# Alternating plain and seven-product k-groups in both feed-forwards, with later flips and 40 low parts made by ACT and an accumulating DMA

## The chip, the cores and the metric

One core of a Trainium2 chip runs the kernel. The metric is the device time in microseconds (us) of one execution; three executions gave a median of 2728.22 us. The profile is of one more execution.

## What is computed

Two transformer-like blocks on 256 tokens of width 2048, all in float32, one after the other. Cut to what the change touches:

```python
def swiglu(h, w_gate, w_up, w_down):                    # first block, hidden width 5632
    return (jax.nn.silu(h @ w_gate) * (h @ w_up)) @ w_down

def conv_glu_ffn(h, w_up, conv_w, conv_b, w_down):      # second block, hidden width 5632
    u = h @ w_up                                        # 2 x 5632 columns
    u = causal_depthwise_conv(u, conv_w) + conv_b       # 3 taps along the tokens
    gate, val = u[..., :5632], u[..., 5632:]
    return (jax.nn.silu(gate) * val) @ w_down
```

The first block is attention and `swiglu`, the second a gated mixer, a cross attention and `conv_glu_ffn`, each with a residual add and an RMS norm in front.

## The kernel before, in words

**Units, tasks and chunks.** Every weight matrix is cut into units of 512 rows by 512 columns (1 MB, one DMA on SP's queue into one of 4 `raw` buffers). The order of all units is fixed beforehand by `plan`. A unit is used as two *tasks* of 256 rows. For each task `split_ahead` makes two tiles: `wh`, the weights rounded to the short float format that TensorE multiplies fast (a cast on ACT, L225), and `wl`, what the rounding left (weights minus `wh`, a subtraction on DVE, L226). There are 5 buffers of each. `task()` calls `split_ahead` three tasks ahead of the one that TensorE takes. One product of activations and weights is three matmuls (`mm`, L270 to L272): high by high, high by low, low by high. A k-group is 512 rows of the shared dimension (4 of 128), a chunk is 512 output columns. An ordinary task is 12 matmuls of 512 columns: 2 row blocks of 128, 2 outputs, 3 matmuls.

**The pair.** In the first feed-forward, chunks 1 to 10 of gate and up are computed together by `pair`. Gate and up columns, token halves and row halves form 2 by 2 blocks. A *plain* k-group costs 48 matmuls in 4 tasks. A *seven-product* k-group does the same block product with 7 instead of 8 products (Strassen's scheme in Winograd's form): 42 matmuls in 7 tasks of 6, but DVE must first form the sums of weights, in place in `raw` (`form`, L242, L243, L244, L246, four instructions), and all 7 operands need their own cast and subtraction. Sums of activations are made once by `differences`. Before the change k-groups 0, 1, 2 are plain and 3 is seven-product. At the end DVE adds the partial products (L359 to L373), ACT applies silu (L787), DVE multiplies (L774), and `group_job` flips the result: TensorE transposes (L405) and a split into high and low part (L387, L388). The second feed-forward uses the ordinary `gemm` for its up chunks, then `conv_job`: flips (L405), taps (L1139, L1140, L1142), silu, product, split.

**What is done when.** TensorE's instructions run in the order of the program text. The order on the other engines is a scheduler's, which takes what is ready. Side jobs (`spawn`) are advanced by `tick`, once after every 6 matmuls of the projections. `group_job` and `conv_job` wait 3 ticks before their first flip. After each part of up chunks (`PARTS1`, `PARTS2`) the down projection of the part before runs: four column chunks n, each adding into `x` (`add_x`, L451).

**Memory.** PSUM has 4 banks `acc`, 3 `aux` (flips, and in `pair` one product each) and one `po`. SBUF tiles come from tags with a fixed number of buffers (`s4` 21, `s2` 12).

Of the kernel before, what the change touches and what calls it, by code (L numbers as in the profile page):

```python
# [83 lines left out]
class _Net:  # L84
# [71 lines left out]
    def units(w, n, ks=range(4)):  # L156
        return [(w, n, k) for k in ks]

    def plan(self):

        p, U = [], self.units
        self.seven = set()
# [10 lines left out]
        def ffn(gate, up, off, down, parts, seven=False):  # L173
            prev = None
            for ks in parts:
                for c in ks:
                    if seven and c:
                        pair(U(gate, c), U(up, c + off))
                    else:
                        add([U(gate, c), U(up, c + off)], c == 0)  # L180
                if prev:
                    add([U(down, n, prev) for n in range(4)])
                prev = ks
            add([U(down, n, prev) for n in range(4)])

        add([U("w_qkv", n) for n in (4, 0, 1, 2, 3)])
        add([U("w_o", n) for n in range(4)], True)
        ffn("w_gate", "w_up1", 0, "w_dn1", PARTS1, True)
# [9 lines left out]
        ffn("w_up2", "w_up2", 11, "w_dn2", PARTS2)  # L198
        return p

    def load_ahead(self, n):
# [10 lines left out]
    def split_ahead(self, n):  # L212

        nc = self.nc
        while self.halves < min(n, len(self.tasks)):
            u, j = self.tasks[self.halves]
            if j < 10:
                self.load_ahead(u + 1)
                raw = self.raws[u][:, 2 * j:2 * j + 2]
            else:  # L220
                raw = self.form(u, j - 10)
            h = self.wp.tile([128, 2, 512], F32R, name=self.nm("wh"), tag="wh", bufs=WBUF)
            l = self.wp.tile([128, 2, 512], F32R, name=self.nm("wl"), tag="wl", bufs=WBUF)
            for m in (slice(0, 1), slice(1, 2)) if u == 0 else (slice(0, 2),):
                nc.scalar.copy(h[:, m], raw[:, m])  # L225
                nc.vector.tensor_sub(l[:, m], raw[:, m], h[:, m].bitcast(F32))  # L226
            self.parts[self.halves] = (h, l)
            self.halves += 1
            if j == 1:
                del self.raws[u]  # L230
                self.load_ahead(u + 1 + RAW)
            elif j == 16:
                del self.raws[u], self.raws[u + 1], raw
                self.load_ahead(u + 2 + RAW)
# [53 lines left out]
                    done(banks[c])  # L288
                self.tick()

    def differences(self, acts):


        nc = self.nc
# [1 line left out]
        for g, z in enumerate(acts):  # L296
# [2 lines left out]
            nc.vector.tensor_add(f, h.bitcast(F32), l.bitcast(F32))  # L299
            p, q = f[:, :, 0:128], f[:, :, 128:256]  # L300
            yield 2
            if g < len(acts) - 1:
                hl = self.s4([128, 2, 4, 128], F32R)
                nc.vector.tensor_sub(p, p, q)
                nc.scalar.copy(hl[:, 0], p)
                nc.vector.tensor_sub(hl[:, 1], p, hl[:, 0].bitcast(F32))
                out.append((hl[:, 0], hl[:, 1]))
            else:
                s = self.s4([128, 8, 128])
                nc.vector.tensor_add(s[:, 0:2], q[:, 0:2], q[:, 2:4])  # L310
                nc.vector.tensor_sub(s[:, 2:4], s[:, 0:2], p[:, 0:2])
                nc.vector.tensor_sub(s[:, 4:6], p[:, 0:2], q[:, 0:2])
                nc.vector.tensor_sub(s[:, 6:8], p[:, 2:4], s[:, 2:4])
                yield 1
                h, l = (self.s4([128, 8, 128], F32R) for _ in range(2))
                nc.scalar.copy(h, s)
                nc.vector.tensor_sub(l, s, h.bitcast(F32))
                out.append((h, l))
            yield 2
        return out  # L320

    def pair(self, left, right, acts, diffs):

        nc = self.nc
        acts = [self.need(z) for z in acts]
        p2, p4, p5, p3 = (self.bank(tag="acc") for _ in range(4))
        last = len(acts) - 1  # L330
        for g in range(last):
            for units in (right, left):
                for k, w in enumerate(self.weights(units[g])):
                    f = g == 0 and k == 0
                    if units is left:
                        self.mm(p2, acts[g], k, 0, w, f, False)
                        self.mm(p4, acts[g], k, 1, w, f, False)
                    else:
                        self.mm(p5, acts[g], k, 1, w, f, False)
                        self.mm(p3, diffs[g], k, 0, w, f, False)  # L340
                    self.tick()
        assert self.stream[self.used:self.used + 2] == [right[last], left[last]]
        self.used += 2
        A, S = acts[last], diffs[last]

        def product(o, z, k, t, start):
            h, l = self.task()
            for i in range(2):
                self.mm(o, z, k + i, t, (h[:, i], l[:, i]), start and i == 0, i == 1)
            self.tick()  # L350

        add = nc.vector.tensor_add
        u, a, b, c = (self.s2([128, 512]) for _ in range(4))
        product(p3, S, 6, 0, False)
        o = self.bank()
        product(o, A, 0, 0, True)
        nc.scalar.copy(u, o)
        product(p2, A, 2, 0, False)
        add(a, p2, u)  # L359
        yield a  # L360
        o = self.bank()
        product(o, S, 2, 0, True)
        add(u, o, u)
        product(p5, S, 0, 0, False)
        add(b, p5, u)
        add(b, p3, b)
        yield b
        o = self.bank(tag="po")
        product(o, S, 4, 0, True)
        add(u, o, u)  # L370
        product(p4, A, 2, 1, False)
        add(c, p4, u)
        add(u, p5, u)  # L373
        yield c
        yield u
# [384 lines left out]
    def swiglu(self):  # L760
        nc, a = self.nc, self.a
        r, xacts = self.r, self.xacts

        def up(c, late):
            silu, hid = [], []

            def on_gate(G):
# [4 lines left out]
            def on_up(U):  # L772
                for t in range(2):
                    nc.vector.scalar_tensor_tensor(silu[t], U[t], r[:, t:t + 1], silu[t],  # L774
                                                   op0=ALU.mult, op1=ALU.mult)
                hid.append(self.spawn(self.group_job(silu)))

            if c == 0:
                self.gemm([(self.units(w, c), f) for w, f in (("w_gate", on_gate), ("w_up1", on_up))],
                          xacts, late=late)  # L780
                diffs.append(self.spawn(self.differences(xacts)))
                return hid[0]
            diffs[0] = self.need(diffs[0])
            U = []
            for i, z in enumerate(self.pair(self.units("w_gate", c), self.units("w_up1", c), xacts, diffs[0])):
# [4 lines left out]
            return hid[0]  # L790

        diffs = []
        self.ffn(up, "w_dn1", PARTS1, lambda *z: self.residual(*z, "g_mix_2"))

    def ffn(self, up, w, parts, last):

        prev = None
        for p in parts:
            hid = [up(c, late=c == 0) for c in p]
            if prev:  # L800
                self.residual(w, *prev, None)
            prev = (p, hid)
        last(w, *prev)


    def mixer(self):
# [320 lines left out]
    def conv_ffn(self):  # L1127
# [16 lines left out]
            return y  # L1144

        def conv_job(c, rows):
            yield 3
            hl = self.group()
            for k in (0, 2):
                yg = conv(rows[0], c, k)  # L1150
# [5 lines left out]
                yield 1  # L1156
            return hl

        def up(c, late):
            rows, hid = [], []  # L1160

            def on_gate(p):
# [2 lines left out]
            def on_val(p):  # L1165
# [1 line left out]
                hid.append(self.spawn(conv_job(c, rows)))  # L1167

            self.gemm([(self.units("w_up2", c + 11 * j), f)
                       for j, f in enumerate((on_gate, on_val))], xacts, late=late)  # L1170
            return hid[0]

        self.ffn(up, "w_dn2", PARTS2, self.final)

    def final(self, w, ks, acts):

# [115 lines left out]
```

## Time and profile before

| what | value |
|---|---|
| median of 3 executions | 2728.22 us (2726.79 to 2728.71) |
| profiled execution | 2726.57 us |
| its span, first to last instruction | 2724.7 us |
| TensorE busy | 2684.9 us (99%) |
| DVE / ACT / POOL busy | 1669.1 / 1354.5 / 27.1 us |
| mean granted TensorE clock | 0.999 of 2.4 GHz |

Matmuls overlap, and their ends are modelled, so a busy TensorE says little; the spacing of what waits for it says more. Idle time of DVE, ACT or the queues costs nothing unless TensorE waits for it. The profiled execution has 1.9 us outside its span.

### The profile page before, as it was taken

How to read it: one execution, taken by the hardware profiler on the slowest of the kernel's cores; microseconds unless marked ns; L12 is line 12 of the kernel's file. 1: busy time of each engine (PE TensorE's matmuls, PEld its weight loads, DVE VectorE, ACT ScalarE, POOL GpSimd, SP SyncE). 2: the span in 40 equal slices, each digit the busy share in tenths (PEclk: the TensorE clock that was granted, in tenths of full speed). 3: DMA queues.
4: the chain of work that ended last, by engine and by line, in shares of the span. 5: the costliest groups of instructions: out<-in, count | busy, mean ns of one | idle time of the engine just before them, and what ended most of it. 6: DMA issues, size and time to landing. Idle time of an engine off the chain costs nothing.

```text
span 2724.7 us, 31400 instructions
## 1 busy us (share of the span) xinstructions
PE 2684.9 (99%) x12472; PEld 2218.8 (81%) x12472; DVE 1669.1 (61%) x1981; ACT 1354.5 (50%) x1775; POOL 27.1 (1%) x27
## 2 busy tenths in 40 slices
PE   8999999999999999999999999999999999999998
PEld 7778888787878888888888888888888888888887
DVE  7775677767676764745545555554565656556565
ACT  6555554444444454544444455444555554554543
POOL 0000000000000000000000000000000000000000
PEclk9999999999999999999999999999999999999999
DMA  7334545555555555445555556444555555555553
GB/s 302 109 124 155 187 166 194 204 178 199 185 193 179 200 185 184 161 164 181 190 188 197 184 206 227 171 158 168 185 186 185 186 185 187 189 191 190 185 201 124
DMA packets 74083, 499.60 MB, mean 183 GB/s; under 512 B 8496, under 2 KB 9392, under 8 KB 14928
## 3 DMA queue, kind: packets, MB, share of 16 engines
q1 hardware_dynamic: 73936, 497.59, 51.1%
q8 instruction: 98, 1.61, 0.2%
q14 instruction: 49, 0.40, 0.0%
HBM read 495.46 MB, written 2.10 MB: 183 GB/s over the span
## 4 chain that ended last, share of the span: by engine, by line
PE 91%; DVE 4%; issue 2%; DMA 1%; ACT 1%; POOL 1%; SPq 0%; DVEq 0%; POOLq 0%; ACTq 0%
PE acc L270 28%; PE acc L272 28%; PE acc L271 28%; PE aux L405 2%; PE po L718 1%; DMA raw<-in_w_qkv 1%; DVE s L774 1%; POOL sm L429 1%; DMA x<-in_x 0%; PE aux L272 0%; PE aux L271 0%; PE aux L270 0%; DVE wl L226 0%; PE aux L949 0%; PE aux L679 0%
## 5 line engine op out<-in xcount | busy, mean ns | idle before, releaser
L226 DVE TENSOR_TENSOR wl<-raw,wh 128x1024 fp32r<-128x1024 f32 (+1 forms) x952 | 1160.7, 1221 | 961.1 <-ACT wh L225 959.4
L225 ACT CAST wh<-raw 128x1024 fp32r<-128x1024 f32 (+1 forms) x952 | 997.8, 1050 | 1175.8 <-PE acc L272 1154.7
L270 PE MATMUL acc<-wh,s 128*128 128x512 f32 x3600 | 1425.5, 396 | 6.5 <-ACT wh L225 5.6
L272 PE MATMUL acc<-wh,s 128*128 128x512 f32 x3600 | 1404.6, 390 | 0.6 <-DVE s L388 0.6
L271 PE MATMUL acc<-wl,s 128*128 128x512 f32 x3600 | 1403.3, 390 | 0.3 <-DVE wl L226 0.3
L270 PEld LDWEIGHTS acc<-wh,s 128*128 128x128 f32 x3600 | 676.9, 188 | 147.2 <-ACT wh L225 5.6
L272 PEld LDWEIGHTS acc<-wh,s 128*128 128x128 f32 x3600 | 676.3, 188 | 144.8 <-DVE s L388 1.1
L271 PEld LDWEIGHTS acc<-wl,s 128*128 128x128 f32 x3600 | 677.4, 188 | 134.2 <-DVE wl L226 1.4
L405 PE MATMUL aux<-con,s 128*128 128x128 f32 x408 | 63.1, 273 | 15.6 <-DVE s L774 15.6
L405 PEld LDWEIGHTS aux<-con,s 128*128 128x128 f32 x408 | 50.2, 140 | 31.5 <-DVE s L774 19.1
L420 ACT ACTIVATE s<-acc,sm 128x512 f32<-128x512 f32 x72 | 48.9, 689 | 33.3 <-PE acc L272 33.3
L451 DVE TENSOR_TENSOR x<-acc,x 128x512 f32<-128x512 f32 x96 | 61.7, 681 | 0.0
L387 ACT CAST s<-aux 128x512 fp32r<-128x512 f32 x66 | 38.3, 584 | 40.3 <-PE aux L405 30.1
L1139 ACT ACTIVATE s<-aux,vec 128x256 f32<-128x256 f32 x88 | 48.1, 560 | 13.5 <-PE aux L405 8.3
L429 POOL TENSOR_TENSOR sm<-sm,mhalf 128x2 f32<-128x2 f32 (+3 forms) x22 | 26.0, 1182 | 2691.2 <-DVE sm L437 2354.3
L388 DVE TENSOR_TENSOR s<-aux,s 128x512 fp32r<-128x512 f32 x66 | 44.7, 685 | 10.5 <-ACT s L387 9.4
L392 ACT ACTIVATE s<-aux,vec 128x256 fp32r<-128x256 f32 x80 | 37.7, 473 | 22.3 <-PE aux L405 13.9
L1140 DVE SCALAR_TENSOR_TENSOR s<-aux,vec,s 128x255 f32<-128x255 f32 x88 | 41.1, 477 | 2.6 <-ACT s L1139 0.2
L393 DVE SCALAR_TENSOR_TENSOR s<-aux,vec,s 128x256 fp32r<-128x256 f32 x80 | 38.2, 481 | 6.7 <-ACT s L392 5.4
L1142 DVE SCALAR_TENSOR_TENSOR s<-aux,vec,s 128x254 f32<-128x254 f32 x88 | 40.1, 477 | 1.2
L692 ACT ACTIVATE s<-s,sm 128x128 f32<-128x128 f32 (+1 forms) x64 | 28.3, 444 | 13.7 <-DVE sm L687 13.7
L426 ACT ACTIVATE s<-x 128x512 f32<-128x512 f32 (+1 forms) x44 | 29.1, 663 | 9.8 <-DVE x L1187 9.3
(194 smaller groups left out, 965.4 us busy)
## 6 DMA issues: line engine op xcount, KB each, us to landing
raw<-in_w_up SPq DMA_DIRECT2D x132, 1024.0 KB, 4.7
raw<-in_w_dn SPq DMA_DIRECT2D x88, 1024.0 KB, 4.8
raw<-in_w_in SPq DMA_DIRECT2D x64, 1024.0 KB, 4.7
raw<-in_w_gate SPq DMA_DIRECT2D x44, 1024.0 KB, 4.7
raw<-in_w_ckv SPq DMA_DIRECT2D x32, 1024.0 KB, 4.7
raw<-in_w_qkv SPq DMA_DIRECT2D x19, 1024.0 KB, 6.0
raw<-in_w_o SPq DMA_DIRECT2D x16, 1024.0 KB, 4.8
raw<-in_w_br SPq DMA_DIRECT2D x16, 1024.0 KB, 4.8
```

Of the source, the lines that this page charges most:

```text
L225: nc.scalar.copy(h[:, m], raw[:, m])
L226: nc.vector.tensor_sub(l[:, m], raw[:, m], h[:, m].bitcast(F32))
L270: nc.tensor.matmul(o, ah[:, k, s], h, start=first, stop=False)
L271: nc.tensor.matmul(o, ah[:, k, s], l, start=False, stop=False)
L272: nc.tensor.matmul(o, al[:, k, s], h, start=False, stop=last)
L388: nc.vector.tensor_sub(l[:, k0:k0 + n], src, h[:, k0:k0 + n].bitcast(F32))
L405: self.nc.tensor.transpose(b[:, j, t * 128:t * 128 + 128], srcs[t][:, (k + j) * 128:(k + j) * 128 + 128], self.ident)
L420: self.nc.scalar.activation(dst[t], pss[t], AF.Identity, bias=0.0, scale=sc[:, t:t + 1])
L429: self.nc.gpsimd.tensor_tensor(out, var, self.mhalf[:, :n], op=ALU.pow)
L451: nc.vector.tensor_add(xs[t], pss[t], xs[t])
L1139: nc.scalar.activation(y[:, j], b[:, j], AF.Identity, bias=bb, scale=w2)
L1140: nc.vector.scalar_tensor_tensor(y[:, j, 1:256], b[:, j, 0:255], w1, y[:, j, 1:256], op0=ALU.mult, op1=ALU.add)
```

## The change

In each feed-forward, chunks 1 to 10 go through `pair`. `SEVEN1 = (1, 3)` names the seven-product k-groups of the first feed-forward, `SEVEN2 = (3,)` those of the second, where there were none. A pair with two such groups keeps three extra PSUM banks (two `aux`, one `po`) from the first to the last of them. Both feed-forwards use the parts of the first, and of the four down chunks n half run after each up chunk of the part, where they ran after all of it. `group_job` and `conv_job` wait 8 ticks in place of 3 before the flip, except for chunk 0. In the second feed-forward chunk 0 stays in `gemm`, and `differences` runs once after it. In each of the 20 pairs two tasks, the second of the first right unit and the second of the first left unit, get their low part otherwise: ACT writes minus the rounded weights (`scalar.mul` by -1), and a DMA issued by POOL adds the weights to it in SBUF. The core of the diff:

```diff
-PARTS1 = ((0,), (1, 2), (3, 4), (5, 6), (7, 8), (9, 10))
-PARTS2 = ((0, 1, 2), (3, 4, 5), (6, 7, 8), (9, 10))
+PARTS = ((0,), (1, 2), (3, 4), (5, 6), (7, 8), (9, 10))
+SEVEN1, SEVEN2 = (1, 3), (3,)
...
+    def ffn_steps():
+        prev = None
+        for ks in PARTS:
+            for i, c in enumerate(ks):
+                yield c, None, None
+                if prev:
+                    for n in range(4 * i // len(ks), 4 * (i + 1) // len(ks)):
+                        yield None, n, prev
+            prev = ks
...
-        def pair(a, b):
+        def pair(a, b, seven):
+            self.by_dma |= {(len(p), 1), (len(p) + 1, 1)}
             for g in range(len(a)):
-                if g == len(a) - 1:
+                if g in seven:
                     self.seven.add(len(p))
                 p.extend((b[g], a[g]))
...
                 nc.scalar.copy(h[:, m], raw[:, m])
-                nc.vector.tensor_sub(l[:, m], raw[:, m], h[:, m].bitcast(F32))
+                if (u, j) not in self.by_dma:
+                    nc.vector.tensor_sub(l[:, m], raw[:, m], h[:, m].bitcast(F32))
+                    continue
+                nc.scalar.mul(l[:, m], raw[:, m], -1.0)
+                nc.gpsimd.dma_start(l[:, m], raw[:, m], accum_op=ALU.add)
...
-            if g < len(acts) - 1:
-                hl = self.s4([128, 2, 4, 128], F32R)
+            if g not in seven:
+                h, l = (self.s2([128, 4, 128], F32R) for _ in range(2))
...
+            if o1 is None:
+                o1, o6, o7 = self.bank(), self.bank(), self.bank(tag="po")
+            end = g == seven[-1]
+            product(p3, S, 6, 0, end)
+            product(o1, A, 0, 0, end)
+            if end:
+                u, a, b, c = (self.s2([128, 512]) for _ in range(4))
+                nc.scalar.copy(u, o1)
+            product(p2, A, 2, 0, end)
+            if end:
+                add(a, p2, u)
+                yield a
...
-                hid.append(self.spawn(self.group_job(silu)))
+                hid.append(self.spawn(self.group_job(silu, wait=3 if c == 0 else 8)))
...
-            yield 3
+            yield 3 if c == 0 else 8
...
+            diffs[0] = self.need(diffs[0])
+            rows = [[], []]
+            for i, z in enumerate(self.pair(self.units("w_up2", c), self.units("w_up2", c + 11),
+                                            xacts, diffs[0], SEVEN2)):
+                nc.scalar.activation(z, z, AF.Identity, bias=0.0, scale=r[:, i // 2:i // 2 + 1])
+                rows[i % 2].append(z)
+            return self.spawn(conv_job(c, rows))
```

## Rows read from the trace of the kernel before

**Rows 1.** Page, parts 1 to 3: busy time, granted clock, DMA queues.
```profile
PE 2684.9 (99%) x12472; PEld 2218.8 (81%) x12472; DVE 1669.1 (61%) x1981; ACT 1354.5 (50%) x1775; POOL 27.1 (1%) x27
PEclk9999999999999999999999999999999999999999
q1 hardware_dynamic: 73936, 497.59, 51.1%
```

**Rows 2.** Waits of TensorE, 300 to 950 us: who waited, total us, times, longest.
```profile
PE aux L405 <- DVE s L774: 15.6, 10, 1.6
```

**Rows 3.** Timeline of ACT, a plain stretch of the first feed-forward: start, us, instruction.
```profile
331.59 1.05 ACT L225 CAST wh<-raw 128x1024 fp32r<-128x1024 f32 x1 [1.67 <-PE acc L272]
334.31 1.05 ACT L225 CAST wh<-raw 128x1024 fp32r<-128x1024 f32 x1 [1.67 <-PE acc L272]
...
345.19 1.05 ACT L225 CAST wh<-raw 128x1024 fp32r<-128x1024 f32 x1 [1.67 <-PE acc L272]
```

**Rows 4.** Timeline at the end of pair 1 and its flip.
```profile
365.84 0.39 PE L272 MATMUL acc<-wh,s 128*128 128x512 f32 x1
366.16 0.50 PE L270 MATMUL acc<-wh,s 128*128 128x512 f32 x1
366.49 0.40 PE L271 MATMUL acc<-wl,s 128*128 128x512 f32 x1
...
369.72 0.27 PE L405 MATMUL aux<-con,s 128*128 128x128 f32 x1
370.75 0.74 DVE L774 SCALAR_TENSOR_TENSOR s<-s,sm,s 128x512 f32<-128x512 f32 x1
371.55 0.55 PE L405 MATMUL aux<-con,s 128*128 128x128 f32 x3 [1.56 <-DVE s L774]
```

**Rows 5.** Groups by line and form, whole span: count, busy us, mean ns, idle before.
```profile
L226 DVE TENSOR_TENSOR wl<-raw,wh 128x1024 fp32r<-128x1024 f32 x948 | 1158.0, 1223 | 958.1 <-ACT wh L225 956.5
L225 ACT CAST wh<-raw 128x1024 fp32r<-128x1024 f32 x948 | 995.3, 1052 | 1172.7 <-PE acc L272 1154.7 <-issue 9.0 <-PE po L272 3.1
L243 DVE TENSOR_TENSOR raw<-raw,raw 128x1024 f32<-128x1024 f32 x10 | 12.3, 1225 | 0.3
L426 ACT ACTIVATE s<-x 128x1024 f32<-128x1024 f32 x4 | 4.2, 1053 | 0.4 <-DMA x<-in_x 0.3
L451 DVE TENSOR_TENSOR x<-acc,x 128x512 f32<-128x512 f32 x96 | 61.7, 681 | 0.0
L1140 DVE SCALAR_TENSOR_TENSOR s<-aux,vec,s 128x255 f32<-128x255 f32 x88 | 41.1, 477 | 2.6 <-ACT s L1139 0.2
L429 POOL TENSOR_TENSOR sm<-sm,mhalf 128x8 f32<-128x8 f32 x8 | 15.9, 1988 | 116.8 <-DVE sm L598 116.8
```

**Rows 6.** Timeline of DVE, first to fourth forming instruction of pair 1.
```profile
347.53 1.22 DVE L242 TENSOR_TENSOR raw<-raw 128x1024 f32<-128x1024 f32 x1
...
353.58 1.23 DVE L246 TENSOR_TENSOR raw<-raw 128x1024 f32<-128x1024 f32 x1
...
360.22 0.69 DVE L359 TENSOR_TENSOR s<-acc,s 128x512 f32<-128x512 f32 x1 [0.43 <-PE acc L272]
```

**Rows 7.** Windows: us, busy (count) of PE, PEld, DVE, ACT, POOL; clock; DMA share; GB/s.
```profile
345.20:372.70 27.50, 25.94 (x116) 20.99 (x115) 24.47 (x26) 15.75 (x17) 0.00 (x0) 1.00 0.43 158
2069.70:2087.20 17.50, 17.50 (x84) 14.51 (x83) 16.20 (x26) 11.44 (x19) 0.00 (x0) 1.00 0.45 162
2020.00:2290.00 270.00, 270.00 (x1239) 223.58 (x1238) 172.08 (x220) 150.24 (x190) 0.00 (x0) 1.00 0.52 185
```

**Rows 8.** DMA issues: tile, count, KB each, median us from issue to landing.
```profile
raw<-in_w_up SPq DMA_DIRECT2D x132, 1024.0 KB, 4.7
out<-x SPq DMA_DIRECT2D x8, 256.0 KB, 2.5
s<-in_pool_m SPq DMA_DIRECT2D x2, 512.0 KB, 5.6
s<-in_g_final SPq DMA_DIRECT2D x2, 512.0 KB, 7.2
```

More of the change, by code (lines that the diff above doesn't have):

```diff
@@ L157, in units @@
         return [(w, n, k) for k in ks]
+    @staticmethod
+    def ffn_steps():
[7 more added lines that the diff above has]
+            prev = ks
     def plan(self):
         p, U = [], self.units
+        self.by_dma = set()
         self.seven = set()
@@ L165, in add, with ffn @@
             p.extend(chunks[c][g] for c, g in self.order(chunks, late))
-        def pair(a, b):
+        def pair(a, b, seven):
+            self.by_dma |= {(len(p), 1), (len(p) + 1, 1)}
             for g in range(len(a)):
-                if g == len(a) - 1:
+                if g in seven:
                     self.seven.add(len(p))
                 p.extend((b[g], a[g]))
[L173 to L184, printed above, removed]
+        def ffn(gate, up, off, down, seven):
+            for c, n, ks in self.ffn_steps():
+                if n is not None:
+                    add([U(down, n, ks)])
+                elif c:
+                    pair(U(gate, c), U(up, c + off), seven)
+                else:
+                    add([U(gate, c), U(up, c + off)], True)
+            add([U(down, n, PARTS[-1]) for n in range(4)])
         add([U("w_qkv", n) for n in (4, 0, 1, 2, 3)])
         add([U("w_o", n) for n in range(4)], True)
-        ffn("w_gate", "w_up1", 0, "w_dn1", PARTS1, True)
+        ffn("w_gate", "w_up1", 0, "w_dn1", SEVEN1)
         add([U("w_in", n) for n in (0, 1)], True)
@@ L197, in plan @@
         add([U("w_co", n) for n in range(4)], True)
-        ffn("w_up2", "w_up2", 11, "w_dn2", PARTS2)
+        ffn("w_up2", "w_up2", 11, "w_dn2", SEVEN2)
         return p
@@ L289, in gemm, with differences @@
                 self.tick()
-    def differences(self, acts):
+    def differences(self, acts, seven):
         nc = self.nc
@@ L301, in differences @@
             yield 2
-            if g < len(acts) - 1:
-                hl = self.s4([128, 2, 4, 128], F32R)
+            if g not in seven:
+                h, l = (self.s2([128, 4, 128], F32R) for _ in range(2))
                 nc.vector.tensor_sub(p, p, q)
-                nc.scalar.copy(hl[:, 0], p)
-                nc.vector.tensor_sub(hl[:, 1], p, hl[:, 0].bitcast(F32))
-                out.append((hl[:, 0], hl[:, 1]))
+                nc.scalar.copy(h, p)
+                nc.vector.tensor_sub(l, p, h.bitcast(F32))
             else:
@@ L317, in differences, with pair, product @@
                 nc.vector.tensor_sub(l, s, h.bitcast(F32))
-                out.append((h, l))
+            out.append((h, l))
             yield 2
         return out
-    def pair(self, left, right, acts, diffs):
+    def pair(self, left, right, acts, diffs, seven):
         nc = self.nc
+        add = nc.vector.tensor_add
         acts = [self.need(z) for z in acts]
         p2, p4, p5, p3 = (self.bank(tag="acc") for _ in range(4))
[L330 to L346, printed above, removed]
+        used = set()
+        def product(o, z, k, t, stop):
@@ L347, in product @@
             h, l = self.task()
             for i in range(2):
-                self.mm(o, z, k + i, t, (h[:, i], l[:, i]), start and i == 0, i == 1)
+                self.mm(o, z, k + i, t, (h[:, i], l[:, i]), id(o) not in used, stop and i == 1)
+                used.add(id(o))
             self.tick()
[L352 to L371, printed above, removed]
+        o1 = None
+        for g in range(len(acts)):
+            A, S = acts[g], diffs[g]
+            if g not in seven:
+                for units in (right, left):
+                    outs = ((p2, A, 0), (p4, A, 1)) if units is left else ((p5, A, 1), (p3, S, 0))
+                    for k, w in enumerate(self.weights(units[g])):
+                        for o, z, t in outs:
+                            self.mm(o, z, k, t, w, id(o) not in used, False)
+                            used.add(id(o))
+                        self.tick()
+                continue
+            assert self.stream[self.used:self.used + 2] == [right[g], left[g]]
+            self.used += 2
+            if o1 is None:
[10 more added lines that the diff above has]
+                yield a
+            product(o6, S, 2, 0, end)
+            if end:
+                add(u, o6, u)
+            product(p5, S, 0, 0, end)
+            if end:
+                add(b, p5, u)
+                add(b, p3, b)
+                yield b
+            product(o7, S, 4, 0, end)
+            if end:
+                add(u, o7, u)
+            product(p4, A, 2, 1, end)
@@ L762, in swiglu, with up @@
         r, xacts = self.r, self.xacts
-        def up(c, late):
+        def up(c):
             silu, hid = [], []
@@ L775, in on_up @@
                                                    op0=ALU.mult, op1=ALU.mult)
-                hid.append(self.spawn(self.group_job(silu)))
+                hid.append(self.spawn(self.group_job(silu, wait=3 if c == 0 else 8)))
             if c == 0:
                 self.gemm([(self.units(w, c), f) for w, f in (("w_gate", on_gate), ("w_up1", on_up))],
-                          xacts, late=late)
-                diffs.append(self.spawn(self.differences(xacts)))
+                          xacts, late=True)
+                diffs.append(self.spawn(self.differences(xacts, SEVEN1)))
                 return hid[0]
@@ L784, in up @@
             U = []
-            for i, z in enumerate(self.pair(self.units("w_gate", c), self.units("w_up1", c), xacts, diffs[0])):
+            for i, z in enumerate(self.pair(self.units("w_gate", c), self.units("w_up1", c),
+                                            xacts, diffs[0], SEVEN1)):
                 if i % 2 == 0:
@@ L792, in swiglu, with ffn @@
         diffs = []
[L793 to L803, printed above, removed]
+        self.ffn(up, "w_dn1", lambda *z: self.residual(*z, "g_mix_2"))
+    def ffn(self, up, w, last):
+        hid = {}
+        for c, n, ks in self.ffn_steps():
+            if n is None:
+                hid[c] = up(c)
+                continue
+            self.gemm([(self.units(w, n, ks), lambda pss: self.add_x(n, pss, None))], [hid[k] for k in ks])
+            if n == 3:
+                for k in ks:
+                    del hid[k]
+        last(w, PARTS[-1], [hid.pop(k) for k in PARTS[-1]])
     def mixer(self):
@@ L1157, in conv_job, with up @@
             return hl
-        def up(c, late):
+        diffs = []
+        def up(c):
             rows, hid = [], []
@@ L1169, in up, with up7, last @@
             self.gemm([(self.units("w_up2", c + 11 * j), f)
-                       for j, f in enumerate((on_gate, on_val))], xacts, late=late)
+                       for j, f in enumerate((on_gate, on_val))], xacts, late=True)
             return hid[0]
-        self.ffn(up, "w_dn2", PARTS2, self.final)
+        def up7(c):
+            if c == 0:
+                hid = up(c)
+                diffs.append(self.spawn(self.differences(xacts, SEVEN2)))
+                return hid
+            diffs[0] = self.need(diffs[0])
[5 more added lines that the diff above has]
+            return self.spawn(conv_job(c, rows))
+        def last(*z):
+            diffs.clear()
+            xacts.clear()
+            self.final(*z)
+        self.ffn(up7, "w_dn2", last)
     def final(self, w, ks, acts):
```

## The prediction

> **What bounds the kernel now.** I read the page first: TensorE is busy 99% of the span at the full granted clock, DVE 61%, ACT 50%, and one DMA queue, SP's, carries the loads; POOL issues none [rows 1]. Busy is not enough, so next the casts in a plain stretch [rows 3]: every cast waits for TensorE to finish a task and give a buffer back, and from 331.59 to 345.19 there are five steps of 2.72 us. A task is 12 matmuls, so one matmul costs 2.72 / 12 = 0.2267 us, and the other engines wait for TensorE. Third, its waits over the first feed-forward [rows 2]: only one kind, a transpose that waits for L774 on DVE, 10 times. In the second feed-forward TensorE is busy 270.0 of 270.0 us [rows 7]. So the time moves with what TensorE executes and with any new wait of TensorE; work on DVE, ACT, POOL and the queues counts only where it comes too late.
>
> **Matmuls removed.** A seven-product group has 42 matmuls, a plain one 48. The first feed-forward goes from 10 seven-product groups to 20, the second from none to 10: 20 x 6 = 120 fewer, at 0.2267 us: **-27.2 us** [rows 3].
>
> **The flip that waited.** At the end of pair 1 the first transpose starts at 369.72, the next at 371.55, right behind the second L774 (370.75 + 0.74) [rows 4]. The step is 1.83 us; a transpose beside others takes (0.55 - 0.27) / 2 = 0.14, so 1.7 us are lost, 10 times: 17 us (the waits view, which counts from the modelled end, says 15.6 [rows 2]; I take 17). With 8 ticks in place of 3 the flip comes 5 x 6 matmuls = 6.8 us later, some 5 us after L774 has ended. Late next would be the hidden group that the flip makes; its first user is chunk 10's, in the last down projection, 16 ticks and one unit after the pair, against 9 ticks for the second flip: 11 ticks, 15 us, cover the split. **-17 us**. In the second feed-forward TensorE did not wait at the flips, so nothing is gained there.
>
> **Ends of pairs.** At 365.84, 366.16, 366.49 the first matmuls behind a pair come 0.32 and 0.33 us apart in place of 0.227 [rows 4]: 0.2 us, while a bank is given back. The second feed-forward gets 10 such ends: **+2 us**.
>
> **DVE and ACT.** A seven-product group needs of DVE 7 subtractions and 4 forming instructions, 7 x 1.223 + 4 x 1.225 = 13.5 us [rows 5], of TensorE 42 x 0.2267 = 9.5: DVE loses 3.9 us. Casts run up to four tasks ahead, 10.9 us, since five buffers exist [rows 3], and before the change this covered it: from the first form at 347.53 on, DVE is ahead, and at 360.22 it waits 0.43 us for TensorE [rows 6]; no matmul waits for a low part [rows 2]. With groups 1 and 3, one plain group lies between: TensorE 10.9, DVE 4 x 1.22 = 4.9, so 6.0 us are won back, more than 3.9. Per up chunk with its two down chunks n, DVE has in the first feed-forward 28 subtractions, 8 forms, 9 adds and products, 2 splits, 4 adds into x: 28 x 1.22 + 8 x 1.225 + 15 x 0.69 = 54.3 us, against TensorE's (180 + 96) x 0.2267 + flips, 64.5 us. In the second: 25 subtractions, 4 forms, 7 adds, 4 adds into x, conv_job's 16 taps at 0.477 and 4 others at 0.69: 53.4 of 65.9 us. ACT gets 60 casts and 40 negations, 105 us over the kernel at 1.05 [rows 5], and 10 x 0.6 of copies: from 50% to about 55%. All of it fits between TensorE's tasks: nothing. If the lead were gone, each additional seven-product group would show its 3.9 us.
>
> The parts add 16 adds into x, 16 x 0.68 = 10.9 us of DVE behind gemms that alternate between two pairs of banks: nothing. The differences of the second feed-forward are some 12 us of DVE once (estimate: 1.22 us per 1024 columns), beside chunk 0, where TensorE has 8 units, 43.5 us, and DVE 16 subtractions, 19.6: nothing. Where 40 subtractions leave DVE, 49 us go there; TensorE did not wait for them: nothing by itself.
>
> **The 40 low parts by DMA.** This is the part that no row shows. A task's buffer comes free 10.9 us before its own first matmul. In that time: cast 1.05, negation 1.05 (an ACTIVATE of the same size takes 1.053 [rows 5]), POOL's issue, the transfer. POOL's issue: not below 0; the nearest POOL instruction takes 1.99 [rows 5]; I take 1.2, between. The transfer: not below 2.5 us, what 256 KB take out of SBUF; 512 KB loads landed after 5.6 and 7.2 us beside the weight loads [rows 8]; it reads two sources, so not above twice 7.2 = 14.4. I take 7.2, as for a crowded one of the same size. Sum 2.1 + 1.2 + 7.2 = 10.5, just under 10.9: **0**. From the ends: 2.1 + 0 + 2.5 = 4.6 (still 0; an earlier landing gains nothing) and 2.1 + 2.0 + 14.4 = 18.5, 7.6 us late. A pair has two such tasks, two tasks apart; if the first stalls TensorE, the second has that much longer, so lateness counts once per pair, 20 times.
>
> The Trainium skill (DMA: Bandwidth & Descriptors, section "Anatomy of one DMA — SWDGE (gpsimd) path") fits a DMA that POOL issues as about 2.0 us plus its bytes at 436 GB/s, an estimate of 3.2 us for 512 KB. By that the path would be 6.5 us and the sum the same; the loads of this trace are dearer than the fit, and no row here shows an accumulating one.
>
> Behind the negation ACT's next casts queue, 1.05 us later, with 1.67 us of idle time before each [rows 3]. On POOL nothing else is queued in the feed-forwards. On SP's queue the load of the fourth unit after waits until the DMA has read `raw`: the second such unit's ends about 10.5 us after its buffer came, 7.8 us into the pair, and its 4.7 us load [rows 8] is in at 12.5; its first cast is due at 16.3 (six tasks of 2.72) at the earliest. The accumulating packets take shares of DMA engines that are half free (0.52 [rows 7]).
>
> **Sum.** 2726.6 (the profiled execution) - 27.2 - 17 + 2 + 0 = 2684.4. The median shown is 1.6 us above that execution, so **2686 us**. What a measurement of this kernel can tell from no change is about 0.2%, 5.5 us.
>
> **Rivals.** *The low part lands late (slower if late enough).* Place: the second task of each pair's first unit, at its second matmul. Price: 20 x lateness. It uses up the gain of 42.2 us at 2.1 us, that is when issue and transfer take 10.9 us in place of 8.4. At 1 us late it gives 2706, at the upper bound 20 x 7.6 = 152, 2838. For it: the margin is 0.4 us, and ACT's casts and conv_job's ACT work can start the negation later. Against: the loads that took 7.2 us stood behind others.
>
> *POOL's issue is held behind DVE.* conv_job keeps DVE busy 16.2 of 17.5 us [rows 7], now from about 10.5 us before the next pair to 7 us into it. If POOL's issue had to wait for its end, a transfer of 7.2 would land 14.2 us into the pair, where 2.7 is due: 11.5 us, 10 pairs, 115 us: 2801. Nothing in this trace shows POOL beside DVE in a feed-forward. The Trainium skill (SBUF — State Buffer, section "Who interferes with whom") says that an instruction of DVE with two inputs in SBUF, as L226 is, and one of GpSimd that reads SBUF block each other, whichever came second. By that rule alone a hold lasts one DVE instruction and not the whole stretch; no row bears on it.
>
> *DVE becomes the bound in the seven-product groups.* For it: 24.47 of 27.50 us busy around the only such group of a pair [rows 7]. If the 20 additional groups showed 3.9 us each: +78, 2764; a quarter of that, 2705. Against: the count above, and the 0.43 us that DVE waited.
>
> *The later flip still waits*, because DVE is behind at the end of a pair: the 17 us stay, 2703. It needs DVE 5 us later than now.
>
> **How the numbers follow.** Everything hidden 0.62 (2677 to 2694, the spread of the small terms). Late landing 0.22: 0.10 up to 2722, 0.02 each between there and "no change" and within it, 0.08 slower. POOL held 0.02, slower. DVE the bound 0.10: 0.04 up to 2722, 0.01 same, 0.05 slower. Flip still waits 0.04. Faster: 0.62 + 0.12 + 0.04 + 0.04 = 0.82; same 0.03; slower 0.08 + 0.02 + 0.05 = 0.15. Within 2677 to 2722: 0.62 + 0.10 + 0.04 + 0.04 = 0.80.
>
> **What would show it.** TensorE's count falls by 120 matmuls to 12352, casts still step by 2.72 us in plain stretches, the wait of L405 for L774 is gone, POOL has 40 DMA issues, L226 falls by 40 and rises by 60 (952 to 972), ACT gets 40 instructions of 1.05 us. Right is a landing under 8.8 us after the negation's end. Wrong would be: the high-by-low matmul (L271 now) waiting for a DMA at the start of pairs, TensorE waiting for L226's successor inside seven-product groups, or gaps at transposes.

## The result, and the profile after

The changed kernel takes 2693.68 us (median of 4, 2690.36 to 2694.69); the kernel before, measured beside it, 2727.51 us (2726.04 to 2728.71). The ratio is 0.9874, 95% interval 0.9857 to 0.9891: 33.8 us faster. The forecast was 2686 with 2677 to 2722, so the sign and the range held, and 7.7 us of the expected gain did not come. The profiled execution took 2693.14 us against 2726.57, 33.4 us less where the sum had 42.2.

The page of the changed kernel, parts 1, 3, 5 and 6; a row of part 5 ends with the engine's idle time before the group and what ended most of it:

```profile
PE 2661.7 (99%) x12352; PEld 2196.2 (82%) x12352; DVE 1847.6 (69%) x2185; ACT 1460.3 (54%) x1889; POOL 62.0 (2%) x67
...
q1 hardware_dynamic: 73936, 497.59, 51.4%
q0 software_dynamic: 5760, 20.97, 4.1%
...
L239 DVE TENSOR_TENSOR wl<-raw,wh 128x1024 fp32r<-128x1024 f32 (+1 forms) x972 | 1183.1, 1220 | 714.9 <-ACT wh L237 703.0
...
L242 POOL DMA_DIRECT2D wl<-raw x40 | 34.8, 871 | 1183.9 <-ACT wl L241 1049.1
...
L241 ACT ACTIVATE wl<-raw 128x1024 fp32r<-128x1024 f32 x40 | 42.3, 1058 | 19.4 <-PE acc L287 19.4
...
wl<-raw POOLq DMA_DIRECT2D x40, 512.0 KB, 5.1
```

Against [rows 1] TensorE has 120 matmuls less, as counted, and POOL and ACT have 40 new instructions each, of 0.87 and 1.06 us. The subtraction (now L239) ran 972 times: 952 - 40 + 60.

The waits of TensorE in the first feed-forward, [rows 2], are gone: from 300 to 950 us the view has no entry at all. In place of the end of pair 1 of [rows 4] the timeline now shows four transposes (L427, before L405) without any idle time:

```profile
375.28 0.39 PE L288 MATMUL acc<-wh,s 128*128 128x512 f32 x1
375.51 0.60 PE L427 MATMUL aux<-con,s 128*128 128x128 f32 x4
375.87 0.48 PE L286 MATMUL acc<-wh,s 128*128 128x512 f32 x1
```

The waits have moved to the second feed-forward, which had none. The same view from 1880 to 2660 us (who waited for what: us in total, times, longest):

```profile
PE acc L287 <- DMA wl<-raw: 2.6, 5, 1.0
PE aux L427 <- DVE s L1168: 1.9, 1, 1.9
PE acc L286 <- ACT s L321: 0.6, 1, 0.6
```

The first row is the high-by-low matmul that waits for an accumulating DMA, the event that the prediction named as a sign against it. The view counts 5, and 2 more stand under the weight loads of the same line (L287 on PEld). By the starts of the matmuls the 7 waits cost 4.0 us and their successors 0.75 more. The second row is the flip of chunk 0, the third the differences of the activations; together 3.0 us. Behind the flip of chunk 0 came a stretch at half clock, 1.7 us by the starts, which the control below does not have; more on that at the end. So the missing 8.8 us lie in one feed-forward: 4.7 + 3.0 + 1.7 by the starts, less 0.6, because the flip wait was worth 17.6 by experiment and not 17.

One pair of the second feed-forward shows why the DMA was late. Timelines of ACT, POOL, SP's queue and TensorE:

```profile
2296.49 1.03 ACT L237 CAST wh<-raw 128x1024 fp32r<-128x1024 f32 x1
...
2299.30 1.06 ACT L241 ACTIVATE wl<-raw 128x1024 fp32r<-128x1024 f32 x1
...
2302.76 1.06 ACT L237 CAST wh<-raw 128x1024 fp32r<-128x1024 f32 x1
...
2304.26 1.05 ACT L241 ACTIVATE wl<-raw 128x1024 fp32r<-128x1024 f32 x1
...
2300.66 0.86 POOL L242 DMA_DIRECT2D wl<-raw  x1 [60.66 <-ACT wl L241]
2305.59 0.86 POOL L242 DMA_DIRECT2D wl<-raw  x1 [4.07 <-PE acc L288]
...
2305.94 9.78 SPq L217 DMA_DIRECT2D raw<-in_w_up  x3
...
2314.82 0.50 PE L287 MATMUL acc<-wl,s 128*128 128x512 f32 x1 [0.99 <-DMA wl<-raw]
```

The DMA view of two windows of it, 2300.5 to 2301.5 and 2305.5 to 2306.5 (KB, us from issue to landing):

```profile
wl<-raw POOLq DMA_DIRECT2D x1, 512.0 KB, 5.1
...
raw<-in_w_up SPq DMA_DIRECT2D x1, 1024.0 KB, 7.0
wl<-raw POOLq DMA_DIRECT2D x1, 512.0 KB, 9.2
```

The first low part is issued at 2300.66 and lands 5.1 us later, at 2305.8. That landing frees its `raw` buffer, and at 2305.94 SP issues the next 1 MB load, 0.35 us after POOL issued the second low part. Side by side the second low part needs 9.2 us and the load 7.0; in the kernel without DMAs, below, a load issued in the same window took 4.9. From its cast (2302.76) to its landing (2314.8) it took 12.0 us: 1.5 to the start of the negation, 1.05 for it, 0.3 to POOL's issue and 9.2 to the landing. The lead of the casts is 10.9. In the seven pairs that waited, 4 to 10, this chain took 11.1 to 12.0 us. In the first feed-forward a low part takes up to 9.4 us too, but no matmul waited there: for that one ACT made the negation (553.98) ahead of the cast (554.94), and it landed 0.3 us before its matmul.

### The profile page after: what moved, and what is told of

Read it like the earlier page. It is cut to its first block, busy times and chain, and to the rows that moved or that the text cites. A ratio compares the mean times of both kernels' runs of the same rounds, so it can differ in the third digit from the quotient of the medians.

```text
span 2691.4 us, 31797 instructions
## 1 busy us (share of the span) xinstructions
PE 2661.7 (99%) x12352; PEld 2196.2 (82%) x12352; DVE 1847.6 (69%) x2185; ACT 1460.3 (54%) x1889; POOL 62.0 (2%) x67
## 3 DMA queue, kind: packets, MB, share of 16 engines
q1 hardware_dynamic: 73936, 497.59, 51.4%
q0 software_dynamic: 5760, 20.97, 4.1%
## 4 chain that ended last, share of the span: by engine, by line
PE 94%; DMA 3%; DVE 2%; ACT 1%; POOL 0%; issue 0%; SPq 0%; POOLq 0%; DVEq 0%; ACTq 0%
PE acc L286 28%; PE acc L287 28%; PE acc L288 28%; DMA wl<-raw 2%; PE aux L427 2%; PE aux L288 1%; PE aux L287 1%; PE aux L286 1%; PE po L740 1%; PE po L287 1%; PE po L288 1%; PE po L286 1%; PE aux L975 0%; POOL sm L451 0%; DMA raw<-in_w_qkv 0%
## 5 line engine op out<-in xcount | busy, mean ns | idle before, releaser
L239 DVE TENSOR_TENSOR wl<-raw,wh 128x1024 fp32r<-128x1024 f32 (+1 forms) x972 | 1183.1, 1220 | 714.9 <-ACT wh L237 703.0
L237 ACT CAST wh<-raw 128x1024 fp32r<-128x1024 f32 (+1 forms) x1012 | 1059.7, 1050 | 1046.2 <-PE acc L288 982.3
L286 PE MATMUL acc<-wh,s 128*128 128x512 f32 x3440 | 1365.1, 397 | 7.9 <-ACT wh L237 5.7
L287 PE MATMUL acc<-wl,s 128*128 128x512 f32 x3440 | 1342.5, 390 | 3.2 <-DMA wl<-raw 2.6
L288 PE MATMUL acc<-wh,s 128*128 128x512 f32 x3440 | 1343.1, 390 | 0.6 <-DVE s L410 0.6
L286 PEld LDWEIGHTS acc<-wh,s 128*128 128x128 f32 x3440 | 647.3, 188 | 146.1 <-DVE s L388 7.1
L288 PEld LDWEIGHTS acc<-wh,s 128*128 128x128 f32 x3440 | 646.7, 188 | 138.2 <-DVE s L410 1.1
L287 PEld LDWEIGHTS acc<-wl,s 128*128 128x128 f32 x3440 | 647.9, 188 | 133.7 <-DMA wl<-raw 5.8
L427 PEld LDWEIGHTS aux<-con,s 128*128 128x128 f32 x408 | 50.2, 140 | 15.8 <-issue 4.1
L427 PE MATMUL aux<-con,s 128*128 128x128 f32 x408 | 60.9, 272 | 1.9 <-DVE s L1168 1.9
L242 POOL DMA_DIRECT2D wl<-raw x40 | 34.8, 871 | 1183.9 <-ACT wl L241 1049.1
L241 ACT ACTIVATE wl<-raw 128x1024 fp32r<-128x1024 f32 x40 | 42.3, 1058 | 19.4 <-PE acc L287 19.4
L286 PE MATMUL aux<-wh,s 128*128 128x512 f32 x120 | 46.7, 389 | 0.0
L287 PE MATMUL aux<-wl,s 128*128 128x512 f32 x120 | 46.7, 389 | 0.0
L288 PE MATMUL aux<-wh,s 128*128 128x512 f32 x120 | 46.7, 389 | 0.0
```

Of the source, the lines that this page charges most:

```text
L241: nc.scalar.mul(l[:, m], raw[:, m], -1.0)
L286: nc.tensor.matmul(o, ah[:, k, s], h, start=first, stop=False)
L287: nc.tensor.matmul(o, ah[:, k, s], l, start=False, stop=False)
L288: nc.tensor.matmul(o, al[:, k, s], h, start=False, stop=last)
L427: self.nc.tensor.transpose(b[:, j, t * 128:t * 128 + 128], srcs[t][:, (k + j) * 128:(k + j) * 128 + 128], self.ident)
```

## The experiments

**The changed kernel once more, and without the DMAs.** The control is the changed kernel itself. The question is whether most of the missing gain is the DMAs', or whether DVE, with 40 subtractions more, becomes the bound in their place.

> The changed kernel once more, as the measure for the other three of this call. It should come out at a ratio of 0.987 to the kernel before, within 0.002, with TensorE's 7 waits for an accumulating DMA in the second feed-forward, some 4 us in total, at the second low part of a pair.

```diff
-            self.by_dma |= {(len(p), 1), (len(p) + 1, 1)}
```

> All 40 low parts are subtractions on DVE again. Theory (DVE has room, and the DMA only brings its own lateness): the 4.7 us of late landings and their echo go, nothing takes their place, 2689, some 0.998 of the changed kernel. Rival (DVE needs the relief at the beginning of a pair, where conv_job and the first forms meet): TensorE waits for low parts of DVE, 0.5 us or more at each of 20 pairs, 10 us or more, 2700 or slower.

The control took 2693.97 us (ratio 0.988, 0.9865 to 0.9895), without the DMAs it is 2686.76 us (0.9854, 0.984 to 0.9869): 7.2 us less. Waits from 1880 to 2660 us, first of the control, then of the kernel without DMAs (its L426 and L1167 are L427 and L1168 above):

```profile
PE acc L287 <- DMA wl<-raw: 3.9, 7, 1.2
...
```

```profile
PE aux L426 <- DVE s L1167: 1.8, 1, 1.8
PE acc L285 <- ACT s L320: 0.6, 1, 0.6
```

No wait for DVE takes the place of the DMA's, though DVE does 40 subtractions more. The windows view of that stretch, control first, agrees (columns: us, busy time and count of PE, PEld, DVE, ACT, POOL, then granted clock, DMA share, GB/s):

```profile
1880.00:2660.00 780.00, 773.59 (x3491) 634.58 (x3490) 584.18 (x704) 455.17 (x556) 17.98 (x21) 1.00 0.59 202
```

```profile
1880.00:2660.00 780.00, 777.56 (x3518) 640.16 (x3517) 610.94 (x730) 440.83 (x542) 0.70 (x1) 1.00 0.53 188
```

In the same 780 us TensorE gets through 27 matmuls more, 27 x 0.2267 = 6.1 us; from 300 to 950 us the counts are 2902 and 2901. The profiled executions differ in the first 300 us as well, ahead of the first pair: 1473 matmuls in the control against 1480, behind a stretch at half clock (17.0 to 20.4 us) that the other does not have. So the DMAs' own cost is 4.7 us in the changed kernel's profiled execution and 6.1 in the control's, all of it in the second feed-forward; the 7.2 hold something else too.

**One DMA per pair, and two in the first unit.** The question is whether the second DMA is late because of the load that the first one's landing releases, or whether an accumulating DMA is late by itself.

```diff
-            self.by_dma |= {(len(p), 1), (len(p) + 1, 1)}
+            self.by_dma |= {(len(p), 1)}
```

> Only the first of the two low parts of a pair is made by the DMA, the second by DVE: 20 DMAs. Theory (the second is late, the first never): all waits of TensorE for an accumulating DMA are gone, 2689. Rival (any accumulating DMA beside conv_job's work is late): some of the first ones are late now, a wait remains in the second feed-forward.

```diff
-            self.by_dma |= {(len(p), 1), (len(p) + 1, 1)}
+            self.by_dma |= {(len(p), 0), (len(p), 1)}
```

> Still two DMAs a pair, but for both halves of the first unit, so that no buffer of raw weights is given back between them and no weight load is set off in front of the second. Theory (the second lands late because a 1 MB load, set off by the landing of the first, goes in front of it): both land about 4.8 us after the negation's end, 8 to 9 us after their cast, no wait of TensorE, 2689. Rival (the second is late because ACT and POOL come to it late, or because two accumulating DMAs follow each other): the second still lands 7 us or more after its negation, and the waits of TensorE remain or grow, 2694 or slower.

One DMA: 2686.51 us (0.9855, 0.9839 to 0.9871), as without any. Two in the first unit, where no load is freed between them: 2692.66 us (0.9874, 0.986 to 0.9889), no better than the change. The landings from 1880 to 2660 us, by the view of the DMA's line, of the changed kernel, of one DMA, and of two in the first unit:

```profile
DMA to landing us min/median/max: 4.5/5.6/9.2
```

```profile
DMA to landing us min/median/max: 4.5/4.6/5.8
```

```profile
DMA to landing us min/median/max: 4.9/6.0/6.5
```

The mechanism holds: alone a low part lands in at most 5.8 us, and without the freed load between the two in at most 6.5. In the second feed-forward no matmul waits for a DMA any more in either kernel (a weight load does once, 0.2 us). But the half of the expectation that said so of the whole kernel missed: in the first feed-forward two waits came, which the changed kernel does not have. Waits from 300 to 950 us of the kernel with both in the first unit, and its SP and POOL timeline at the first of them:

```profile
PE acc L287 <- DMA wl<-raw: 4.3, 2, 2.2
```

```profile
370.02 0.33 SPq L217 DMA_DIRECT2D raw<-in_w_gate  x1
...
370.62 1.82 POOL L242 DMA_DIRECT2D wl<-raw  x2 [53.76 <-PE acc L288]
```

There a load that was due anyway is issued 0.6 us ahead of two accumulating DMAs back to back. The first of the two lands after 7.9 us, and its matmul waits 2.1 us (2.2 at the other pair). ACT has a part in it: the negation began 4.5 us after the cast (364.75 and 369.28). Pairs 2 and 3 of the second feed-forward tell the two apart. There the negation began 4.6 us after the cast, and again two DMAs followed each other, 1.6 us apart, but the load was issued 1.9 us ahead: the first landed in 5.6 and 5.2 us, and its matmul was late by at most 0.1 us. In the changed kernel a single low part, issued 0.6 us behind a load (874.00 and 873.39), took 8.3 us as well, with no second DMA behind it. So on top of a late negation it is the load issued in the same microsecond that decides, whichever event releases it; moving the tasks only moves the meeting.

**The later flip alone**, on the kernel before:

```diff
-                hid.append(self.spawn(self.group_job(silu)))
+                hid.append(self.spawn(self.group_job(silu, wait=3 if c == 0 else 8)))
```

> The kernel before with one change: the flips of chunks 1 to 10 of the first feed-forward come 8 ticks after their pair, not 3. Theory (TensorE stood 1.7 us at each of 10 flips, for an operand that is ready 5 us earlier than the later flip): 17 us less, 2710, ratio 0.9937, and no wait of a transpose for L774. Rival (the wait only moves, to the flip's later place or to what needs the flipped rows): within 5 us of before.

2709.75 us (0.9938, 0.9925 to 0.995): 17.6 us less, with no wait left in the first feed-forward.

**One seven-product group in place of two** in the first feed-forward, without the DMAs:

```diff
-SEVEN1, SEVEN2 = (1, 3), (3,)
+SEVEN1, SEVEN2 = (3,), (3,)
```

> The change without its DMAs, and in the first feed-forward only k-group 3 with seven products: 60 matmuls more than the version with no DMA, and 8.6 us less work of DVE per pair. Theory (every matmul counts 0.2267 us, DVE's work is hidden): 13.6 us more than the version with no DMA, 2700, ratio 0.990. Rival (the second seven-product group of a pair costs waits on DVE that eat part of its gain): the difference is under 10 us.

2700.9 us (0.9905, 0.989 to 0.992), 14.1 above the kernel without DMAs; 60 matmuls at 0.2267 are 13.6.

**The two groups side by side**, without the DMAs. It tests whether the plain group between them is what gives DVE its lead back:

```diff
-SEVEN1, SEVEN2 = (1, 3), (3,)
+SEVEN1, SEVEN2 = (2, 3), (3,)
```

> The change without its DMAs, with the two seven-product groups of a pair of the first feed-forward side by side (groups 2 and 3 in place of 1 and 3); the number of matmuls stays. Theory (the plain group between them wins back the lead that a seven-product group costs): DVE now falls 2 x 3.9 us behind in a row, and all four buffers of raw weights are held by the first of the two, so TensorE waits inside the second, 1 to 3 us at each of 10 pairs: 2697 to 2717, ratio 0.989 or above. Rival (the lead covers both, the order of the groups means nothing): 2687, as with no DMA, and no new wait.

2719.64 us (0.9971, 0.996 to 0.9983): 33 us above the order 1, 3, for the same work. Waits from 300 to 950 us, and TensorE's timeline at one of each (L286 and L285 are L287 and L286 of the changed kernel):

```profile
PE acc L285 <- DVE s L387: 16.0, 10, 1.6
PE aux L286 <- DVE wl L238: 7.6, 10, 0.8
```

```profile
360.53 0.50 PE L286 MATMUL aux<-wl,s 128*128 128x512 f32 x1 [0.77 <-DVE wl L238]
...
368.60 0.50 PE L285 MATMUL acc<-wh,s 128*128 128x512 f32 x1 [1.60 <-DVE s L387]
```

Inside the second group TensorE now waits for a subtraction, and behind the pair it waits for a bank that DVE's late additions still hold: DVE's timeline has no idle time from 346.94 to 371, no matmul of the stretch waits for a load, and DVE enters the end of the pair behind. Ten pairs pay some 3.3 us each, near the 3.9 that the prediction priced for a lost lead.

**Chunk 0's flip later**, without the DMAs:

```diff
-            yield 3 if c == 0 else 8
+            yield 8
```

> The change without its DMAs, and chunk 0 of the second feed-forward flips after 8 ticks too. Theory (the 2 us that a flip of chunk 0 waits for a bank, and 0.9 us at the first differences, come from conv_job, the differences and the first low parts meeting on DVE and ACT): both waits shrink or go, 2684 against 2686.8. Rival (the differences are late by themselves): the 0.9 us stay, and conv_job's later work delays low parts in the first seven-product group: no gain.

2685.92 us (0.985, 0.9837 to 0.9864), 0.8 less than without it, too little for the timing to resolve; by the starts of the matmuls the second feed-forward is 1.7 us shorter. The waits view from 1880 to 2660 us has one row left, so the flip's wait is gone and the differences' is not:

```profile
PE acc L285 <- ACT s L320: 0.6, 1, 0.6
```

**A second seven-product group in the second feed-forward too**, without the DMAs, and then with one DMA per pair:

```diff
-SEVEN1, SEVEN2 = (1, 3), (3,)
+SEVEN1, SEVEN2 = (1, 3), (1, 3)
```

> The change without its DMAs, and also in the second feed-forward k-groups 1 and 3 with seven products: 60 matmuls fewer than the version with no DMA. DVE's work per chunk there comes to some 64.4 us (53.4 + 2.4 + 8.6), TensorE's to 64.5. Theory (a lead of four tasks covers DVE as long as its sum fits): up to 13.6 us less, 2673, ratio 0.980. Rival (DVE becomes the bound): TensorE waits for low parts inside the first seven-product group of a pair, 1 us or more at each, and the time is 2680 or above.

> Two seven-product groups a pair in both feed-forwards, and the first of the two low parts of each pair by ACT and the accumulating DMA (20 DMAs). Where DVE's sum reaches TensorE's, taking 1.2 us a pair from DVE should pay if anything does. Theory (the waits left in that version come from conv_job meeting the first forms after a short down part, in pairs 2 and 3 alone, and the low part that moves is not what is late there): within 2 us of the same version without DMAs, 2679. Rival (DVE is the bound there): its 5.1 us of flips and 1.0 us of low parts waiting for DVE shrink by half or more, 2675.

2678.94 us (0.9824, 0.981 to 0.9837) and 2678.99 us (0.9825, 0.9811 to 0.9838), the two fastest here and not to be told apart. Of 13.6 us for 60 more matmuls saved, 7.8 came; by the starts of the matmuls 8.8 came in the second feed-forward. The rest of the difference, up to 1.8 us, lies in the first 300 us of the profiled execution, as in the control. Waits from 1880 to 2660 us of the first of the two, and its window from 2020 to 2290:

```profile
PE aux L426 <- DVE s L1167: 4.5, 3, 1.7
PE acc L285 <- ACT s L320: 0.6, 1, 0.6
PE po L286 <- DVE wl L238: 0.6, 2, 0.3
```

```profile
2020.00:2290.00 270.00, 266.05 (x1198) 217.69 (x1197) 256.26 (x296) 169.03 (x200) 0.00 (x0) 1.00 0.53 198
```

DVE is busy 256 of 270 us, and the transposes wait for conv_job's taps (L1167). These waits stand at chunk 0's flip and in pairs 2 and 3, which follow a short down part. From 2140 to 2600 us DVE is busy 428.8 of 460 us, and TensorE 459.96: there two seven-product groups a pair cost no wait at all. With 10 subtractions moved off DVE the time is the same.

**The same with earlier flips of chunks 1 and 2**, meant to take those waits away; the edit also sets chunk 0's flip from 3 to 8 ticks:

```diff
-SEVEN1, SEVEN2 = (1, 3), (3,)
+SEVEN1, SEVEN2 = (1, 3), (1, 3)
...
-            yield 3 if c == 0 else 8
+            yield 5 if c in (1, 2) else 8
```

> Two seven-product groups a pair in both feed-forwards, no accumulating DMA, chunk 0 of the second feed-forward flips after 8 ticks, chunks 1 and 2 after 5, whose next pair comes soon. Theory (the 5 us of flips waiting for DVE come from conv_job reaching into the first seven-product group of the next pair): they go, 2674, ratio 0.9805, faster than both kernels. Rival (DVE has no room left there, the waits move to low parts): 2678 or more.

2682.16 us (0.9835, 0.9821 to 0.9848), 3.2 above the version without it. Waits from 1880 to 2660 us:

```profile
PE aux L426 <- DVE s L1167: 3.7, 3, 1.9
PE aux L285 <- DVE s L1167: 3.0, 2, 1.5
PE acc L286 <- DVE wl L238: 0.9, 2, 0.5
...
```

Two settings changed, and the trace tells them apart. Chunk 0's flip now meets the first seven-product group of pair 1, which wants the `aux` banks for its own products (second row, and 1.9 us of the first): by the starts of the matmuls this kernel loses 3.8 us against the other up to the end of pair 1, and that is the whole loss. The flips of chunks 1 and 2 wait 1.8 us where they waited 3.3, and the low parts behind them 1.1 where it was 0.6; at pair 4 it is 3.4 us behind. So the earlier flips gained little, and the waits moved in part to low parts, as the rival says. The two chunks' setting with chunk 0 left at 3 ticks was not run.

## Why the prediction was right, and where it was not

**Matmuls removed: right.** The count is 12352, and the experiment with 60 more matmuls is 14.1 us slower, where the price says 13.6.

**The flip that waited: right.** Priced at 17, measured 17.6 alone. "Late next would be the hidden group", and nothing waited for it.

**Ends of pairs: right in size.** In the second feed-forward ten ends show two steps each, 0.10 and 0.11 us above 0.227: 2.1 us for 2.

**DVE and ACT covered: right for the subtractions and casts.** The kernels with 20 and with 40 subtractions more on DVE take the same time, 2686.5 and 2686.8 us, and no subtraction is waited for in either feed-forward. The reason held as well: the plain group between two seven-product groups returns the lead, and side by side the same groups cost 33 us. DVE was near to being the bound all the same: with one more group per pair in the second feed-forward 5.8 of 13.6 us did not come by time, 4.8 by the trace of that stretch, and the new waits are all for DVE, none behind pair 3.

**The 40 low parts: the step that failed.** The sum put them at 0; they cost 7.2 us by time, 4.7 and 6.1 us by the traces of two executions. The lead was as the prediction had it, 10.9 us, and the margin of 0.4 us was the weak place. Issue and transfer took 5.1 us together in the median, for 8.4 in the sum (1.2 + 7.2), but 8.3 to 9.2 in the seven pairs that waited. What failed was that the low parts were put as one chain for one task. First, "In that time: cast 1.05, negation 1.05" let the negation follow the cast at once, but ACT has other work: in the pair shown it started 2.8 and 1.5 us after the cast's start, and POOL's issue began another 0.3 us behind its end. Second, "The accumulating packets take shares of DMA engines that are half free" took an average over 270 us; the load is issued within 0.4 us of the DMA, released by the first one's landing. SP's queue was followed for what the DMA delays there, and not for what SP's load does to the DMA. Third, the place: "the second task of each pair's first unit" was on time, the second unit's was late. It "has that much longer" only if the first stalls TensorE, and the first did not.

**Chunk 0 and the differences: "nothing" was 2.8 us.** The prediction set DVE's sum beside TensorE's, and the sum fits; but the flip of chunk 0 comes at a fixed tick, and at that tick DVE had not done the conv taps (L1168), which read the `aux` bank that the next transposes need, and an ACT copy of the differences was late too. Setting the flip later took its wait away in the trace, 1.85 us, for 1.7 net; what delays the differences, 0.93 us, was not tried.

**The rivals.** The late low part was the true one in kind, at a sixth of the price that would have cost the gain. POOL held behind DVE: false. From 2293 to 2311, a stretch in which DVE is busy 15.83 of 18 us, POOL's two issues took 0.86 us each, and each of the 40 began 0.3 us after its negation had ended. The Trainium skill (SBUF — State Buffer, section "Who interferes with whom") has DVE's two-input instructions in SBUF and a GpSimd instruction that reads SBUF block each other, but in its own probe such a subtraction did not stall a DMA. No hold is seen here either, where POOL issues a DMA and the 40 issues lie between 0.86 and 1.05 us. The later flip did not wait.

The parts, by experiment for the flip and the DMAs, by count and price for the matmuls, by the trace for the rest: -17.6 (flip) - 27.2 (matmuls) + 2.1 (ends) + 7.2 (DMAs) + 2.8 (chunk 0) = -32.7, against -33.8 measured.

**Luck.** The measured 2693.68 us lies 0.3 us inside the 2677 to 2694 that the prediction gave to "Everything hidden", though the low parts and chunk 0 were not hidden: the number held better than the account.

## What to carry to other kernels

An operation moved from a busy engine that nobody waits for to a DMA takes on the DMA queues' timetable: follow in the trace which load is issued in the microsecond in which the new transfer runs, and what releases it, not the mean share of the engines. Where one group of work costs an engine more time than it gives, put a group that returns the time behind it; the order alone was worth 33 us here. Here the simpler version was as fast as any: no DMAs, and one more seven-product group in the second feed-forward. And set a sum of work beside the places where it must be done: two such groups a pair cost nothing from pair 4 on, but TensorE waited in pairs 2 and 3, which follow a short down part.

## What the runs showed of the hardware

**An accumulating DMA from SBUF to SBUF** costs the engines about twice what a load costs per byte: 20.97 MB took 4.1% of their span and 497.59 MB 51.4%, 0.196 against 0.103 per MB. With no load in flight beside it 512 KB landed in 4.5 to 5.2 us (13 landings of the kernel with one DMA per pair), with one issued within 0.4 us in 8.3 to 9.2 (the seven pairs that waited). The Trainium skill (DMA: Bandwidth & Descriptors, section "Anatomy of one DMA — SWDGE (gpsimd) path") fits 2.0 us plus the bytes at 436 GB/s, an estimate of 3.2 us for this size; no landing here was that fast.

**Half clock behind a wait of 2 us, in some executions and not in others.** In the profiled execution of the change and in that of the control TensorE waited the same 2.0 us at chunk 0's flip. The same window in both, the change first:

```profile
2001.90:2005.30 3.40, 3.40 (x10) 2.70 (x9) 2.74 (x6) 2.99 (x5) 0.00 (x0) 0.52 0.00 0
```

```profile
2001.90:2005.30 3.40, 3.40 (x18) 2.83 (x16) 2.63 (x6) 3.39 (x6) 0.00 (x0) 1.00 0.12 48
```

The granted clock was 0.52, near the lower level of 1.2 GHz, and 10 matmuls were done where the control did 18 at 2.4 GHz: 1.7 us by the starts of the matmuls that belong to no wait. The kernel with both DMAs in the first unit had it too, behind the same wait at the same flip:

```profile
2006.20:2009.50 3.30, 3.30 (x11) 2.72 (x9) 2.53 (x6) 3.07 (x6) 0.00 (x0) 0.50 0.00 0
```

So it came in two of the seven profiled executions that have this wait of about 2 us. Why the same wait lowered the clock in these and not in the others is open. Near the start, behind TensorE's first waits (5.2 and 1.2 us in the control), six of the thirteen profiled executions ran at half clock for a stretch, the control among them (17.0 to 20.4 us). Such stretches alone move one execution against another by up to 1.8 us.
